# LayerNorm by a square root on ScalarE, pinned transposes and a shared last norm in a two-layer decoder trunk

## The chip, the core and the metric

The kernel runs on one core of one Trainium2 chip. A core has four compute engines, each with its own in-order instruction stream: TensorE (PE in the profile, with its weight loads as PEld) multiplies matrices into PSUM, VectorE (DVE) does elementwise work and statistics, ScalarE (ACT) does activations, scaled copies and casts, GpSimd (POOL) does a little elementwise work and issues DMAs. SyncE (SP) issues most DMAs. The engines meet through semaphores only. The metric is the device time of one execution in microseconds (us); the time before is the median of three runs.

## What is computed

Two layers over a sequence of 512 positions and a model width of 1024, in float32. Layer 0 mixes tokens with gated linear attention (GLA), layer 1 with a gated DeltaNet (GDN); a gated ConvFFN of inner width 2816 follows each. Every sublayer ends in the same way, so there are four LayerNorms:

```python
def layer_norm(x, g, b):
    xf = x.astype(jnp.float32)
    mu = jnp.mean(xf, -1, keepdims=True)
    var = jnp.mean(jnp.square(xf - mu), -1, keepdims=True)
    return ((xf - mu) * lax.rsqrt(var + LN_EPS)).astype(x.dtype) * g + b

h = x
for i in range(DEPTH):                       # DEPTH = 2
    y = gla_mixer(...) if i == 0 else gdn_mixer(...)
    h = layer_norm(ALPHA * h + y, ln_g[i, 0], ln_b[i, 0])
    h = layer_norm(ALPHA * h + conv_ffn(h, ...), ln_g[i, 1], ln_b[i, 1])
return h
```

## The kernel before

**Data and tiles.** The residual stream `h` is kept by token: four token blocks (`tb` 0 to 3) of 128 tokens, each in two halves (`hf`) of 512 columns, so a tile is 128 x 512. The input of every projection, `xh` and `xl`, is the same data transposed (features in the partitions), split in a rounded high part and a remainder; weights are split in the same way (`wh`, `wl`), and each product is three fast matmuls: high by high, high by low, low by high. `fm` products give the output by feature (128 features x 512 tokens), `tm` products by token.

**Stages.** GLA, its output projection and first LayerNorm; FFN of layer 0 and its LayerNorm; GDN, output projection and LayerNorm; FFN of layer 1 and the last LayerNorm, whose result goes to the output. A LayerNorm in the middle (`ln`, L698) normalizes a token block, transposes it on TensorE in eight 128 x 128 pieces (`tr4` into an `xT` bank), and writes `xh` and `xl` for the next stage. The next stage starts with four weight items on token blocks 0 and 1 alone and then does their second halves, so blocks 2 and 3 may come later. The last one (`ln_out`, L752) works in place: subtract the mean and multiply by the gain in one VectorE instruction (L757), scale and add the bias in a second (L758), for each half, then a DMA to the output (L759) on SP's queue.

**The statistics.** `ln_stats` (L680) takes mean and variance from `bn_stats` and `bn_aggr`, and gets the inverse square root on VectorE alone: a first value by integer arithmetic on the bits (L690), and three Newton steps of two instructions each (L693, L694) on 128 x 1 operands. It is one chain of nine small instructions, each of which needs the one before.

**Weights.** A plan lists every weight tile in the order of use. `prefetch` (L350) issues items up to `look` ahead of the one in use: SP's DMA into one of three `raw` buffers, ScalarE's rounding cast (L331, L276, L316) and VectorE's remainder (L332, L277, L317). Ordinary items are held to four at a time; the last projection of an FFN (`last_proj`, L864) keeps all its weights in 16 slots (`wsh`, `wsl`) instead. The letter `l` in the order of the FFN's last part raises `look` from 3 to 8; before, it stands ahead of the last four items.

**The last projection.** Token block by token block and half by half, four 128-row pieces of three matmuls each, 24 matmuls for a block. After a half VectorE adds the product to `h` (L879) and takes statistics (L880). After a block, its LayerNorm is spawned as a task.

**Order.** The program is traced once in Python; a running estimate `clk` of TensorE's time decides where in the trace a waiting task (a generator) goes on: `yield x` means not before x us of that estimate. Then a scheduler orders each engine's instructions; it may let an instruction pass earlier ones that it takes to be later. `keep_in_program_order` pins an instruction behind the one traced just before it on its engine. `pin` holds for the first projections of GLA alone, so the later transposes and matmuls are free. `table` puts ScalarE instructions that need a table of functions in one order among themselves; GLA's and the FFN's functions are not in that chain.

Of the kernel before, what the change touches and what calls it, by code (L numbers as in the profile page):

```python
# [42 lines left out]
CONV_DELAY = 6.0  # L43
COLS_DELAY = 64.0
# [9 lines left out]
def blk(i, n=P):  # L54
    return slice(i * n, i * n + n)


class Trunk:
# [3 lines left out]
    def __init__(self, ctx, tc):  # L62
# [117 lines left out]
    def tr(self, out, a, n=P):  # L180
        self.clk += 0.11
        t = self.nc.tensor.transpose(out, a, self.ident[:n, :n])  # L182
        if self.pin:
            self.tc.keep_in_program_order(t)

    def tr4(self, out, a):
        for j in range(4):
            self.tr(out[:, blk(j)], a[:, blk(j)])
# [248 lines left out]
    def tm_terms(self, ps, ah, al, wh, wl, first, last):  # L437
        self.mm(ps, ah, wh, first, False)
        self.mm(ps, ah, wl, False, False)
        self.mm(ps, al, wh, False, last)  # L440
# [239 lines left out]
    def ln_stats(self, tb):  # L680
        nc = self.nc
        mv = self.small([P, 2], "ln_mv")
        nc.vector.bn_aggr(mv, self.st[tb])
        hv = self.small([P, 1], "ln_var")
        nc.vector.tensor_scalar(hv, mv[:, 1:2], LN_EPS, 0.5, op0=ALU.add, op1=ALU.mult)

        rs = self.small([P, 1], "ln_rs")
        t = self.small([P, 1], "ln_t")
        ri = rs.bitcast(I32)
        nc.vector.tensor_scalar(ri, hv.bitcast(I32), -0.5, float(0x5F3759DF - 0x400000 - (1 << 31)),  # L690
                                op0=ALU.mult, op1=ALU.add)
        for _ in range(3):
            nc.vector.scalar_tensor_tensor(t, rs, hv, rs, ALU.mult, ALU.mult)  # L693
            nc.vector.scalar_tensor_tensor(rs, t, 1.5, rs, ALU.subtract, ALU.mult)  # L694
        self.vec(2.0)
        return mv, rs

    def ln(self, tb, spill=False):  # L698
# [53 lines left out]
    def ln_out(self, tb, out):  # L752
        nc = self.nc
        gb, h = self.ln_gb(), self.h[tb]
        mv, rs = self.ln_stats(tb)
        for hf in range(2):
            nc.vector.scalar_tensor_tensor(h[hf], h[hf], mv[:, 0:1], gb[hf], ALU.subtract, ALU.mult)  # L757
            nc.vector.scalar_tensor_tensor(h[hf], h[hf], rs, gb[2 + hf], ALU.mult, ALU.add)  # L758
            nc.sync.dma_start(out[blk(tb), blk(hf, S)], h[hf])  # L759
        yield 0.0  # L760
# [67 lines left out]
    def ffn(self, cw, li, g, b, final, out=False):  # L828
# [3 lines left out]
        for p0, p1 in CHUNKS + (PLAIN,):  # L832
# [31 lines left out]
    def last_proj(self, xs, final):  # L864
# [52 lines left out]
    def gates(self, nw, width, sg):  # L917
# [50 lines left out]
    def gla(self, li, g, b):  # L968
# [10 lines left out]
        def lr_done(ps):  # L979
            self.exp_ln_table()  # L980
# [154 lines left out]
    def mixer_out(self, y, li, g, b, final=None):  # L1135
# [6 lines left out]

        self.out_proj(a, NC, True, self.ln)
# [37 lines left out]
    def gdn(self, li, g, b):  # L1181
# [17 lines left out]
        def ba_done(ps):  # L1199
            self.exp_ln_table()  # L1200
# [410 lines left out]
```

## Time and profile before

| what | value |
|---|---|
| median of three runs | 1275.92 us (1275.64, 1279.84, 1275.92) |
| the profiled execution's own time | 1275.38 us |
| its span, first to last instruction | 1273.7 us |
| TensorE clock granted, mean | 0.997 of full |
| table loads on ScalarE | 10, of 1283 ns each |
| DMA traffic | 159.07 MB, mean 125 GB/s |

The profile page gives each engine's busy time and the costliest groups of instructions; other views of the same trace list the waits, the chain of work that ended last, or all instructions of an engine in order of time. A row of the time line gives the start in us, the duration in us, engine, source line, operation, output and inputs by the program's names, and in square brackets the idle time of the engine before it and what ended it. Source lines are those of the kernel printed above; L171 is the helper that issues every matmul and L182 the one that issues every transpose, so the tile's name (`fm`, `tm`, `xT`) tells which it is. Durations of TensorE's matmuls overlap: a 512-column matmul shows 0.39 us, but they follow each other every 0.227 us.

### The profile page before, as it was taken

What the parts mean: (1) busy time and instruction counts of PE and PEld (TensorE: products, weight loads), DVE (VectorE), ACT (ScalarE), POOL (GpSimd) and SP (SyncE); (2) the same over time, 40 slices, a digit from 0 to 9 for tenths busy, and PEclk for the clock granted to TensorE, in tenths of its full rate; (3) what the DMA queues carried; (4) which work ended last, traced back from release to release, by engine and by line L of the source; (5) the groups of instructions that cost most, each with busy time, mean ns of one, the idle gap of its engine ahead of it and who ended that gap; (6) DMA issues with size and microseconds to landing.
All of it is one profiled execution on the core that took longest, in us unless ns stands there. A gap on an engine that the chain in (4) does not pass through costs nothing.

```text
span 1273.7 us, 17779 instructions
## 1 busy us (share of the span) xinstructions
PE 1248.6 (98%) x6558; PEld 1049.4 (82%) x6558; DVE 872.3 (68%) x1704; ACT 612.4 (48%) x1176; POOL 153.0 (12%) x226
## 2 busy tenths in 40 slices
PE   8999999999999999999999999999999999999996
PEld 6878888988888888888888878888898888888885
DVE  3683366588667666686789955569777766766678
ACT  3553443554454544445766544443554454554440
POOL 4000000012201201101013130010011211211200
PEclk9999999999999999999999999999999999999998
DMA  7422224069757757742344331143249766756821
GB/s 184 114 71 66 67 84 148 2 151 223 171 132 181 155 129 182 162 130 73 100 145 112 110 95 34 60 124 91 75 108 217 158 160 155 162 150 151 212 83 66
DMA packets 182646, 159.07 MB, mean 125 GB/s; under 512 B 18328, under 2 KB 141786, under 8 KB 182560
## 3 DMA queue, kind: packets, MB, share of 16 engines
q1 hardware_dynamic: 161728, 114.05, 30.2%
q0 software_dynamic: 19440, 42.06, 18.0%
q10 hardware_dynamic: 1392, 1.84, 0.4%
q8 instruction: 51, 0.84, 0.3%
q14 instruction: 35, 0.29, 0.1%
HBM read 141.65 MB, written 5.78 MB: 116 GB/s over the span
## 4 chain that ended last, share of the span: by engine, by line
PE 83%; DVE 6%; DMA 2%; ACT 1%; issue 1%; DVEq 0%; ACTq 0%; SPq 0%
PE fm L171 44%; PE tm L171 30%; PE o L171 2%; PE R L171 1%; PE xT L182 1%; PE V L171 1%; DVE conv L1176 1%; DVE wl L332 1%; PE vn L171 1%; PE pg L171 1%; PE yT L182 1%; PE qkT L182 1%; PE s L171 0%; PE qs L171 0%; PE ks L171 0%
## 5 line engine op out<-in xcount | busy, mean ns | idle before, releaser
L171 PE MATMUL fm<-xh,wh 128*128 128x512 f32 (+1 forms) x1104 | 406.0, 368 | 0.7 <-ACT wh L331 0.7
L171 PE MATMUL fm<-xl,wh 128*128 128x512 f32 (+1 forms) x1104 | 402.5, 365 | 0.0
L171 PE MATMUL fm<-xh,wl 128*128 128x512 f32 (+1 forms) x1096 | 398.8, 365 | 2.6 <-DVE wl L332 2.6
L332 DVE TENSOR_TENSOR wl<-raw,wh 128x1024 fp32r<-128x1024 f32 (+1 forms) x134 | 162.5, 1214 | 142.7 <-ACT wh L331 141.5
L171 PEld LDWEIGHTS fm<-xh,wl 128*128 128x128 f32 x1096 | 206.2, 189 | 36.6 <-DVE wl L332 3.2
L171 PEld LDWEIGHTS fm<-xh,wh 128*128 128x128 f32 x1104 | 208.1, 188 | 34.2 <-ACT wh L331 1.6
L331 ACT CAST wh<-raw 128x1024 fp32r<-128x1024 f32 (+1 forms) x134 | 139.9, 1045 | 199.9 <-PE fm L171 109.8
L171 PEld LDWEIGHTS fm<-xl,wh 128*128 128x128 f32 x1104 | 208.2, 189 | 32.1
L825 DVE SCALAR_TENSOR_TENSOR conv<-fm,ffn_cw,conv 128x511 f32<-128x511 f32 (+1 forms) x176 | 131.0, 745 | 16.5 <-ACT conv L823 14.5
L276 ACT CAST wh<-wq 128x512 fp32r<-128x512 f32 x126 | 74.7, 619 | 107.0 <-PE fm L171 37.4
L277 DVE TENSOR_TENSOR wl<-wq,wh 128x512 fp32r<-128x512 f32 x126 | 84.7, 685 | 56.5 <-ACT wh L276 56.0
L234 POOL DMA_DIRECT2D wq<-in_ffn_w_out_dram x72 | 63.0, 902 | 260.6 <-DVE wl L277 152.1
L171 PE MATMUL tm<-wh,gh 128*128 128x512 f32 x216 | 84.0, 389 | 0.0
L171 PE MATMUL tm<-wl,gh 128*128 128x512 f32 x216 | 84.0, 389 | 0.0
L171 PE MATMUL tm<-wh,gl 128*128 128x512 f32 x216 | 84.0, 389 | 0.0
L171 PE MATMUL tm<-wh,xh 128*128 128x512 f32 x192 | 80.2, 418 | 1.0 <-ACT qk L992 1.0
L171 PE MATMUL tm<-wh,xl 128*128 128x512 f32 x192 | 75.3, 392 | 0.0
L171 PE MATMUL tm<-wl,xh 128*128 128x512 f32 x192 | 75.1, 391 | 0.0
L327 POOL DMA_DIRECT2D wl<-raw x20 | 17.2, 858 | 443.4 <-ACT wl L326 426.9
L531 DVE TENSOR_TENSOR h<-h,tm 128x512 f32<-128x512 f32 x68 | 44.8, 681 | 36.1 <-PE tm L171 36.1
L823 ACT ACTIVATE conv<-fm,ffn_cw 128x512 f32<-128x512 f32 x88 | 59.8, 682 | 0.0
L1176 DVE SCALAR_TENSOR_TENSOR conv<-fm,gdn_cw,conv 128x509 f32<-128x509 f32 (+2 forms) x72 | 53.3, 744 | 1.3 <-ACT conv L1174 0.7
(297 smaller groups left out, 1859.1 us busy)
## 6 DMA issues: line engine op xcount, KB each, us to landing
raw<-in_ffn_w_in_dram SPq DMA_DIRECT2D x88, 512.0 KB, 4.8
wq<-in_ffn_w_out_dram SPq DMA_DIRECT2D x72, 256.0 KB, 5.6
wq<-in_ffn_w_out_dram POOLq DMA_DIRECT2D x72, 256.0 KB, 4.8
raw<-in_gdn_w_in_dram SPq DMA_DIRECT2D x32, 512.0 KB, 4.1
raw<-in_gla_w_in_dram SPq DMA_DIRECT2D x23, 512.0 KB, 3.7
wl<-raw POOLq DMA_DIRECT2D x20, 512.0 KB, 4.7
raw<-in_gla_w_out_dram SPq DMA_DIRECT2D x8, 512.0 KB, 3.6
h<-in_ln_b_dram POOLq DMA_DIRECT2D x16, 256.0 KB, 7.3
```

The costliest lines, as they stand in the source:

```text
L171: t = self.nc.tensor.matmul(out, a, b, start=start, stop=stop, skip_group_check=open_group)
L182: t = self.nc.tensor.transpose(out, a, self.ident[:n, :n])
L234: nc.gpsimd.dma_start(t[i], quad(i, r, col), accum_op=ALU.add)
L276: nc.scalar.copy(wh, t)
L277: nc.vector.tensor_sub(wl, t, wh)
L327: nc.gpsimd.dma_start(wl.bitcast(F32), raw, accum_op=ALU.add)
L331: nc.scalar.copy(wh[:, cols], raw[:, cols])
L332: nc.vector.tensor_sub(wl[:, cols], raw[:, cols], wh[:, cols])
L531: nc.vector.tensor_tensor(h, h, banks[bank][j], op)
L823: nc.scalar.activation(a, ps, AF.Identity, scale=tap(2))
L825: nc.vector.scalar_tensor_tensor(a[:, d:], ps[:, :S - d], tap(2 - d), a[:, d:], ALU.mult, ALU.add)
L1176: self.conv = nc.vector.scalar_tensor_tensor(a[:, d:], ps[:, :S - d], tap(3 - d), a[:, d:], ALU.mult, ALU.add)
```

## The change

- **Statistics.** ScalarE takes the square root of the variance plus epsilon (a Sqrt activation whose bias is a new constant tile `eps`); VectorE takes the reciprocal and refines it by one Newton step instead of three. The estimate for the tasks (`vec`) is 1.2 in place of 2.0.
- **Tables.** The function table that has Sqrt is loaded ahead of each LayerNorm: before `out_proj` in both mixers, and before the last projection of both FFNs. Gelu, and Silu of the gates, join the `table` chain.
- **Order.** The transposes of `ln` and all matmuls of `last_proj` are pinned behind what is traced before them on TensorE. The transposes are traced 1.2 us of the estimate after the block is due (`LN_LAG`) instead of 0.2.
- **Weights.** The letter `l` stands ahead of the last eight items of the FFN instead of the last four.
- **The end.** For token blocks 0 and 1 the last LayerNorm is divided anew: ScalarE normalizes both halves (scale and bias), VectorE multiplies by the gain, a DMA on GpSimd's queue adds the bias row from DRAM, and SP's DMA writes the output. Blocks 2 and 3 stay as they were.

```diff
+LN_LAG = 1.2
...
+        self.eps = ones[:, 2:3]
         nc.gpsimd.memset(ones, 1.0)
+        nc.gpsimd.memset(self.eps, LN_EPS)
...
-    def tr(self, out, a, n=P):
+    def tr(self, out, a, n=P, order=False):
         self.clk += 0.11
         t = self.nc.tensor.transpose(out, a, self.ident[:n, :n])
-        if self.pin:
+        if self.pin or order:
             self.tc.keep_in_program_order(t)
...
-    def exp_ln_table(self):
-        load = self.nc.scalar.preload_act_table_set("natural_log_exp_and_others")
+    def act_table(self, name="natural_log_exp_and_others"):
+        load = self.nc.scalar.preload_act_table_set(name)
         self.tc.keep_in_program_order(load)
         self.table(load)
...
-        hv = self.small([P, 1], "ln_var")
-        nc.vector.tensor_scalar(hv, mv[:, 1:2], LN_EPS, 0.5, op0=ALU.add, op1=ALU.mult)
-
-        rs = self.small([P, 1], "ln_rs")
-        t = self.small([P, 1], "ln_t")
-        ri = rs.bitcast(I32)
-        nc.vector.tensor_scalar(ri, hv.bitcast(I32), -0.5, float(0x5F3759DF - 0x400000 - (1 << 31)),
-                                op0=ALU.mult, op1=ALU.add)
-        for _ in range(3):
-            nc.vector.scalar_tensor_tensor(t, rs, hv, rs, ALU.mult, ALU.mult)
-            nc.vector.scalar_tensor_tensor(rs, t, 1.5, rs, ALU.subtract, ALU.mult)
-        self.vec(2.0)
+        rs, hv, t = (self.small([P, 1], x) for x in ("ln_rs", "ln_var", "ln_t"))
+        self.table(nc.scalar.activation(rs, mv[:, 1:2], AF.Sqrt, bias=self.eps))
+        nc.vector.tensor_scalar(hv, mv[:, 1:2], LN_EPS, -0.5, op0=ALU.add, op1=ALU.mult)
+        nc.vector.reciprocal(rs, rs)
+        nc.vector.scalar_tensor_tensor(t, rs, hv, rs, ALU.mult, ALU.mult)
+        nc.vector.scalar_tensor_tensor(rs, t, 1.5, rs, ALU.add, ALU.mult)
+        self.vec(1.2, self.clk + 1.6)
         return mv, rs
...
-        yield ready - self.clk + 0.2
+        yield ready - self.clk + LN_LAG
         for hf in range(2):
             ps = self.psum("xT")
-            self.tr4(ps, h[hf])
+            self.tr4(ps, h[hf], True)
...
         mv, rs = self.ln_stats(tb)
+        if tb < 2:
+            nb = self.small([P, 1], "ln_nb")
+            nc.vector.scalar_tensor_tensor(nb, mv[:, 0:1], -1.0, rs, ALU.mult, ALU.mult)
+            for hf in range(2):
+                nc.scalar.activation(h[hf], h[hf], AF.Identity, bias=nb, scale=rs)
+                nc.vector.tensor_mul(h[hf], h[hf], gb[hf])
+                nc.gpsimd.dma_start(h[hf], self.gb_rows[1][blk(hf, S)].partition_broadcast(P), accum_op=ALU.add)
+                nc.sync.dma_start(out[blk(tb), blk(hf, S)], h[hf])
+            return
...
-                    nc.scalar.activation(a, a, AF.Gelu)
+                    self.table(nc.scalar.activation(a, a, AF.Gelu))
...
-            self.fm_items(items, steps, order[:-4] + "l" + order[-4:] if plain else order)
+            self.fm_items(items, steps, order[:-8] + "l" + order[-8:] if plain else order)
...
         self.drain()
+        self.act_table("sqrt_and_others")
         self.ln_begin(li, g, b)
...
-                    self.tm_terms(ps, *(t[:, blk(tb)] for t in xs[c]), *ws[hf][c], c == 0, c == n - 1)
+                    self.tm_terms(ps, *(t[:, blk(tb)] for t in xs[c]), *ws[hf][c], c == 0, c == n - 1, True)
...
-                nc.scalar.activation(t, ps, AF.Silu)
+                self.table(nc.scalar.activation(t, ps, AF.Silu))
...
+        self.act_table("sqrt_and_others")
         self.out_proj(a, NC, True, self.ln)
```

More of the change, by code (lines that the diff above doesn't have):

```diff
@@ L178, in vec, with tr4 @@
         return self.dve
-    def tr(self, out, a, n=P):
+    def tr(self, out, a, n=P, order=False):
         self.clk += 0.11
         t = self.nc.tensor.transpose(out, a, self.ident[:n, :n])
-        if self.pin:
+        if self.pin or order:
             self.tc.keep_in_program_order(t)
-    def tr4(self, out, a):
+    def tr4(self, out, a, order=False):
         for j in range(4):
-            self.tr(out[:, blk(j)], a[:, blk(j)])
+            self.tr(out[:, blk(j)], a[:, blk(j)], order=order)
     def mm4(self, out, a, b):
@@ L434, in fm_items, with tm_terms @@
             raise RuntimeError
[L437 to L440, printed above, removed]
+    def tm_terms(self, ps, ah, al, wh, wl, first, last, order=False):
+        self.mm(ps, ah, wh, first, False, order=order)
+        self.mm(ps, ah, wl, False, False, order=order)
+        self.mm(ps, al, wh, False, last, order=order)
     def tm_half(self, a, n, tail, done, slots=False):
@@ L979, in lr_done @@
         def lr_done(ps):
-            self.exp_ln_table()
+            self.act_table()
             nc.scalar.copy(lr[:96, :], ps[:96, :])
@@ L1199, in ba_done @@
         def ba_done(ps):
-            self.exp_ln_table()
+            self.act_table()
             self.table(nc.scalar.activation(ba[:8, :], ps[:8, :], AF.Exp, scale=-1.0))
```

## The prediction

> **What bounds the kernel now.** The page first (engines, share of the span), then the view of TensorE's waits, then the end in order of time.
>
> ```profile
> span 1273.7 us, 17779 instructions
> PE 1248.6 (98%) x6558; PEld 1049.4 (82%) x6558; DVE 872.3 (68%) x1704; ACT 612.4 (48%) x1176; POOL 153.0 (12%) x226
> ...
> PE xT L182 <- DVE h L708: 2.9, 2, 2.7
> PE xT L182 <- DVE ln_rs L694: 0.6, 1, 0.6
> PE tm L171 <- ACT gh L573: 0.2, 1, 0.2
> ```
>
> TensorE is busy for 98% of the span. The change takes no matmul away, so only time in which TensorE stands can be won: 1273.7 - 1248.6 = 25.1 us. Of the waits listed, those at a LayerNorm (transposes `xT`, and one cast at the last projection) are 2.9 + 0.6 + 0.2 = 3.7 us. The largest other part is the end:
>
> ```profile
> 1261.89 0.39 PE L171 MATMUL tm<-wsh,gl 128*128 128x512 f32 x1
> ...
> 1268.98 1.42 DVE L758 SCALAR_TENSOR_TENSOR h<-h,ln_rs,gb 128x512 f32<-128x512 f32 x2
> ...
> 1217.40 5.44 PE tm L171 x24
> ...
> 1255.00:1260.00 5.00, 5.00 (x19) 1.00 0.00 0
> 1260.00:1265.00 5.00, 5.00 (x16) 1.00 0.28 105
> 1265.00:1270.00 5.00, 4.79 (x14) 0.58 0.28 105
> ```
>
> The last matmul ends at 1262.28, VectorE's last instruction at 1270.40, the span at 1273.7: TensorE is done 11.4 us before the end, and VectorE fills nearly all of the stretch (5.00, 5.00 and 4.79 us of 5). Its last result leaves by DMA in the remaining 3.3 us, which the change leaves alone. So two things can be won: at most 3.7 us inside, and VectorE's backlog at the end. The profiled execution took 1275.38 us, 0.54 below the median of 1275.92; 1.7 us of it lie outside the span. I work against 1275.38.
>
> **The end.** VectorE's groups over 1246 to 1274 (busy us, mean ns), and the nearest rows for what is new:
>
> ```profile
> L757 DVE SCALAR_TENSOR_TENSOR h<-h,ln_mv,gb 128x512 f32<-128x512 f32 x8 | 5.9, 741 | 0.0
> L758 DVE SCALAR_TENSOR_TENSOR h<-h,ln_rs,gb 128x512 f32<-128x512 f32 x8 | 5.6, 747 | 0.1
> L880 DVE BATCH_NORM_STATS2 ln_st<-h 128x6 f32<-128x512 f32 x7 | 4.8, 690 | 0.1
> L879 DVE TENSOR_TENSOR h<-h,tm 128x512 f32<-128x512 f32 x7 | 4.7, 675 | 1.3 <-PE tm L171 1.3
> L693 DVE SCALAR_TENSOR_TENSOR ln_t<-ln_rs,ln_var 128x1 f32<-128x1 f32 x12 | 2.5, 209 | 0.1
> L694 DVE SCALAR_TENSOR_TENSOR ln_rs<-ln_t,ln_rs 128x1 f32<-128x1 f32 x12 | 1.8, 153 | 0.2
> L683 DVE BATCH_NORM_AGGREGATE ln_mv<-ln_st 128x2 f32<-128x12 f32 x4 | 0.8, 209 | 0.1
> ...
> L1269 DVE RECIPROCAL gd_bp<-gd_bp 128x4 f32<-128x4 f32 x8 | 1.3, 172 | 0.1
> L744 DVE TENSOR_TENSOR h<-h,gb 128x512 f32<-128x512 f32 x16 | 10.8, 684 | 1.4 <-DMA gb<-in_ln_g_dram 1.4
> L707 ACT ACTIVATE h<-h,ln_nb,ln_rs 128x512 f32<-128x512 f32 x12 | 9.8, 818 | 30.4 <-DVE ln_nb L706 30.3
> L1209 ACT ACTIVATE gd_ea<-gdn_al 8x1 f32<-8x1 f32 x1 | 0.2, 187 | 0.0
> ```
>
> A token block costs VectorE now (4.8 + 4.7) / 7 x 2 = 2.7 us of adds and statistics, (5.9 + 5.6) / 4 = 2.9 of normalizing, (2.5 + 1.8) / 4 = 1.1 of Newton steps, 0.2 for L683 and 0.3 for two more small ones (taken like L694): 7.2 us, while TensorE brings a block every 5.44. Hence the backlog. Afterwards the small chain is one instruction for the variance (0.15), the reciprocal (0.17), 0.21 and 0.15: 0.7. Blocks 0 and 1 pay 2.7 + 0.2 + 0.7 + 0.16 + two multiplications like L744, 1.36: 5.1 us, under TensorE's 5.44. Blocks 2 and 3 pay 2.7 + 0.2 + 0.7 + 2.9 = 6.5.
>
> The halves of the last projection end every 2.72 us, so block 2's first half is there at 1262.28 - 3 x 2.72 = 1254.1. What VectorE still owes block 1 by then I put at 1.4 us (its small chain, ScalarE's 0.82 and the two multiplications begin at about 1252.8), and VectorE isn't idle after: 1254.1 + 1.4 + 2 x 6.5 = 1268.5 against 1270.40, a gain of **1.9 us**. The bounds: no backlog at all when TensorE ends, then block 3's own chain after its second half is 1.4 + 0.2 + 0.7 + 2.9 = 5.2 and VectorE ends at 1267.4, a gain of 3.0; or the scheduler leaves gaps where VectorE waits for ScalarE, half of it, 0.8. The Sqrt isn't in the trace; the 0.19 us of L1209 is the nearest (a 128 x 512 activation, 0.82, the upper end), and VectorE has block work to put under it. ScalarE does nothing at the end now, so the two 0.82 us normalizations for each block are free there. The bias adds of blocks 0 and 1 and the four outputs are weighed as a rival.
>
> **Start of GDN.** TensorE's longest wait in the change's reach:
>
> ```profile
> 565.32 0.50 PE L171 MATMUL tm<-wsh,gh 128*128 128x512 f32 x1 [0.18 <-ACT gh L573]
> 574.27 0.39 PE L171 MATMUL tm<-wsh,gl 128*128 128x512 f32 x1
> 577.35 1.09 PE L182 MATMUL xT<-ident,h 128*128 128x128 f32 x8 [2.69 <-DVE h L708]
> ...
> 565.93 0.68 DVE L574 TENSOR_TENSOR gl<-conv,gh 128x512 fp32r<-128x512 f32 x1
> 573.08 0.20 DVE L683 BATCH_NORM_AGGREGATE ln_mv<-ln_st 128x2 f32<-128x12 f32 x1
> 574.70 0.69 DVE L879 TENSOR_TENSOR h<-h,tm 128x512 f32<-128x512 f32 x1
> 576.75 0.54 DVE L708 TENSOR_SCALAR h<-h,ln_mv,ln_rs 128x512 f32<-128x512 f32 x1
> ```
>
> Block 0's statistics are done at 573.28, its normalized half at 577.29: 4.0 us, because nine small instructions alternate with block 1's adds and statistics. With the Sqrt the chain alone is 0.25 for ScalarE and the hand-over, 0.6 for the reciprocal and one step, 0.16 and 0.54: done at about 574.9, or 576.3 if two of block 1's 0.69 us instructions stand between. The pins take something back: today TensorE runs past the products that need `gl`, written at 566.61; pinned, it stands there from about 565.8, 0.8 us, and reaches the transposes at 575.4 and not at 574.66. So they start at 575.4 to 576.3 and not at 577.35: a gain of 1.0 to 1.9, I take **1.4**. `LN_LAG` decides the place in TensorE's order: behind block 1's 24 matmuls, where the row shows the transposes already.
>
> **Start of the second FFN.**
>
> ```profile
> 903.11 0.63 PE L182 MATMUL xT<-ident,h 128*128 128x128 f32 x4 [0.56 <-DVE ln_rs L694]
> 899.38 0.21 DVE L683 BATCH_NORM_AGGREGATE ln_mv<-ln_st 128x2 f32<-128x12 f32 x1
> 902.42 0.54 DVE L708 TENSOR_SCALAR h<-h,ln_mv,ln_rs 128x512 f32<-128x512 f32 x1
> ```
>
> Here the chain takes 899.38 to 902.96; the short one, even with two 0.69 us instructions between, 3.1 us and so half a microsecond less. TensorE was free at 902.55: the wait of 0.56 goes, **0.6**. After GLA no transposes wait long enough to be listed: 0.
>
> **Weights sooner: 0.** The first of these loads is asked for long before its cast:
>
> ```profile
> 525.87 0.53 SPq L302 DMA_DIRECT2D raw<-in_ffn_w_out_dram  x1
> raw<-in_ffn_w_out_dram SPq DMA_DIRECT2D x8, 512.0 KB, 3.9
> ...
> 550.72 0.62 ACT L276 CAST wh<-wq 128x512 fp32r<-128x512 f32 x1 [4.07 <-issue]
> 551.83 1.65 ACT L316 CAST wsh<-raw 128x512 fp32r<-128x512 f32 x3
> ```
>
> The cast at 551.83 is 26 us behind the issue, and the median landing takes 3.9, so the load isn't late: the cast stands behind L276, and that one for a buffer. Only four ordinary items may be held, and the extra items of `look` come after those, so the letter moves little: the casts are traced one item sooner. Were they to fill ScalarE's gap of 4.07 us, VectorE's work ahead of block 0's statistics would shrink and the rest of the 2.69 could go; the bounds are 0 and 1.3, and a slot taken sooner could delay a convolution by one 0.69 us instruction. I take 0, as the queue's order is kept.
>
> **Tables.** Four loads more, on an engine that is 52% idle:
>
> ```profile
> 2.21 1.28 ACT L638 ACT_TABLE_LOAD   x1 [2.21 <-issue]
> 3.51 0.19 ACT L638 COPY one<-one 128x1 f32<-128x1 f32 x1
> ```
>
> A load costs 1.28 us, and the copy follows 0.02 us after. Its cover is ScalarE's idle time; if one stands ahead of the cast of `gh` (565.32, where TensorE waits already) it costs up to 1.28 there once. The Trainium skill, "ScalarE: Activation LUTs", section "What ACT_TABLE_LOAD costs", adds a drain of 1380 ns to the load's 1283; the row of the copy shows none, and by the page that one misplaced load would cost 2.66, an estimate.
>
> **Sum.** 1.9 + 1.4 + 0.6 = 3.9 us: 1275.38 - 3.9 = **1271.5**.
>
> **The rivals.**
> - *What is won inside is given back.* The pins hold TensorE at `gl` and at transposes that come too soon, and only the end is won: 1275.4 - 1.9 = 1273.5. For it: the 0.8 us above; against: the chain is shorter by four instructions everywhere.
> - *All of it.* The 3.7 us inside go whole and the end gains 3.0, about 6.5 in all: 1268.9. It needs the casts in the gap and a well-chosen order on VectorE.
> - *Slower: the Sqrt stands in ScalarE's queue.* Between stages ScalarE runs eight scaled copies for a block in a row:
>
> ```profile
> 235.16 2.90 ACT L717 ACTIVATE xf<-xT,lb,lg 128x128 f32<-128x128 f32 x8 [0.46 <-PE xT L182]
> ...
> DMA to landing us min/median/max: 5.9/7.3/10.3
> ```
>
> A Sqrt behind such a run is 2.9 us late; VectorE's queue stands at the reciprocal, and pinned transposes make TensorE stand too. It decides from where the delay exceeds the chain's saving of about 1 us and the half-stage of cover; at worst 2.9 after GLA and after GDN: 1275.4 + 5.8 - 3.3 = 1277.9. Against it: block 3's copies there end near the time at which the old chain ended.
> - *The output queue.* SP's queue is in order, and blocks 2 and 3 leave behind block 1, which now waits for its bias add: multiplied at about 1256, landed at 1263 (7.3, the median of the row of landings above, for these adds of the bias in earlier norms) to 1266.3 (10.3), before block 3's first half at 1267.8. Only past that does it cost; landed at 1270, it gives about 1274. The Trainium skill, "SBUF — State Buffer", section "Who interferes with whom", says that a VectorE instruction in a two-port mode locks GpSimd out, descriptors included, so that these adds would land later; no row here shows the last stretch with them.
> - *It doesn't do what it says*: the order on VectorE is again the limit, 1275.4.
>
> **How the numbers follow.** Forecast 0.57, given back 0.20, all of it 0.12, Sqrt in the queue 0.06, output queue 0.03, unchanged 0.02. About 0.5% is what a measurement of this kernel can tell from no change: 1269.5 to 1282.3 around the median. Faster than that are the second rival and the forecast's lower edge, 0.15; slower only if the queue costs more than worked out, 0.03; same 0.82. The range takes in both ends of the end's gain (0.8 to 3.0) and of the inside (0 to 3.7), up to the unchanged case and a median half a microsecond above the profiled run: 1268.0 to 1276.0.
>
> **What would show it.** VectorE's last instruction ends at about 1266.5 (1268.5 less the 2.0 won before); the wait at the start of GDN falls from 2.7 to 1 to 2 us in all (the part at `gl` is new), that at 903 is gone; nine small instructions are five, with a Sqrt of about 0.2 us. Wrong would be: new waits of TensorE for ScalarE, transposes that stand over 1 us elsewhere, outputs of blocks 2 and 3 issued late behind block 1.

## The result and the profile after

The changed kernel took 1267.04 us (median of 6 runs, 1266.18 to 1269.06), the kernel before, run beside it, 1275.78 (median of 6, 1274.37 to 1279.84). The ratio is 0.9929, with a 95% interval of 0.9914 to 0.9944: faster by 0.7%, 8.7 us. The forecast was 1271.5, a gain of 3.9, and its range of 1268.0 to 1276.0 does not hold the time. The profiled execution of the changed kernel took 1266.89 us, its span is 8.5 us shorter than that of before.

The page after, engines and span:

```profile
span 1265.2 us, 17748 instructions
PE 1247.4 (99%) x6558; PEld 1049.5 (83%) x6558; DVE 863.3 (68%) x1638; ACT 624.2 (49%) x1200; POOL 155.3 (12%) x231
```

And the whole view of TensorE's waits (total, times, longest, in us):

```profile
PE warm L629 <- POOL reset L87: 2.0, 1, 2.0
PE fm L174 <- DVE wl L335: 1.8, 2, 1.3
PE cols L185 <- DMA rows<-in_gdn_conv_w_dram: 1.1, 1, 1.1
PE qkT L185 <- ACT conv L1187: 1.1, 2, 0.7
PE tm L174 <- ACT qk L1000: 1.0, 1, 1.0
PE V L174 <- DMA T<-dinvt: 0.8, 1, 0.8
PE R L174 <- issue: 0.6, 1, 0.6
PE tm L174 <- DVE gl L577: 0.3, 1, 0.3
```

The reader is to see what is missing: no transposition `xT` waits any more. Of the 3.7 us of waits at the LayerNorms, 0.3 is left, at `gl`, where the pins were expected to cost 0.8.

To place the gain, TensorE's instructions were counted in the order of their starts; there are 6558 in every profile. The stages below are the times between the starts of two of them: "GLA's norm" from the 1001st to the 1401st, "GDN" (FFN's last projection, its LayerNorm and the start of GDN) from the 2501st to the 2901st, "second FFN" (GDN's output projection, its norm, the FFN's start) from the 4701st to the 5061st. "Start" is the start of the 161st, long before any LayerNorm, and "end" runs from the start of the last product to the end of the span.

| us | start | GLA's norm | GDN | second FFN | end | span |
|---|---|---|---|---|---|---|
| before | 30.71 | 66.91 | 81.60 | 63.92 | 11.77 | 1273.7 |
| changed | 29.37 | 66.51 | 78.69 | 62.69 | 9.30 | 1265.2 |
| gain | 1.34 | 0.40 | 2.91 | 1.23 | 2.47 | 8.5 |
| forecast | 0 | 0 | 1.4 | 0.6 | 1.9 | 3.9 |

The columns leave out the stretches in between, which agree within 0.1 us in these two profiles. Every part of the forecast is too small, GDN the most. The time line of the changed kernel at the start of GDN, TensorE first and then VectorE:

```profile
564.14 0.50 PE L174 MATMUL tm<-wsh,gl 128*128 128x512 f32 x1 [0.34 <-DVE gl L577]
572.67 0.60 PE L185 MATMUL xT<-ident,h 128*128 128x128 f32 x4
...
568.87 0.21 DVE L686 BATCH_NORM_AGGREGATE ln_mv<-ln_st 128x2 f32<-128x12 f32 x1
570.16 0.54 DVE L706 TENSOR_SCALAR h<-h,ln_mv,ln_rs 128x512 f32<-128x512 f32 x1
```

Block 0's chain now takes 568.87 to 570.70 where it took 573.08 to 577.29: it is 2.4 us shorter, and it also begins 4.2 us sooner, of which the stages ahead explain only 1.7 (0.40 and the start's 1.34). So something ahead of the statistics has gone too, and the small chain cannot be the reason. The transposes begin at 572.67 without a wait, 2 us after their input.

### The profile page after: what moved, and what is told of

It reads as the page before. It is cut to its first block, busy times and chain, and to the rows that moved or that the text cites. A ratio compares the mean times of both kernels' runs of the same rounds, so it can differ in the third digit from the quotient of the medians.

```text
span 1265.2 us, 17748 instructions
## 1 busy us (share of the span) xinstructions
PE 1247.4 (99%) x6558; PEld 1049.5 (83%) x6558; DVE 863.3 (68%) x1638; ACT 624.2 (49%) x1200; POOL 155.3 (12%) x231
## 4 chain that ended last, share of the span: by engine, by line
PE 87%; DVE 4%; ACT 1%; DMA 1%; issue 0%; DVEq 0%; ACTq 0%; SPq 0%
PE fm L174 46%; PE tm L174 31%; PE o L174 2%; PE R L174 1%; PE xT L185 1%; PE V L174 1%; DVE conv L1185 1%; DVE wl L335 1%; PE vn L174 1%; PE pg L174 1%; PE yT L185 1%; PE qkT L185 1%; PE s L174 0%; PE qs L174 0%; PE ks L174 0%
```

## The experiments

Each kernel is the one named with the edit shown (e12 has two); all were run in five rounds beside the kernel before. This table has the stages of their profiles (us), the median of the times and the ratio to before; the text goes through them. The same kernel profiled again (e1 and the changed one; e5 and before) shows the three inner stages and the end within 0.1 us, so these are read to a tenth or two, and far better than the times can be. The table has no column for the stretch from the second FFN's to the last product: it takes 332.5 to 332.7 us, but 332.9 in e2 and in e8 and 333.1 in e11.

| run | start | GLA's norm | GDN | second FFN | end | median | ratio, 95% interval |
|---|---|---|---|---|---|---|---|
| e1 changed, again | 28.20 | 66.50 | 78.62 | 62.66 | 9.30 | 1265.78 | 0.9930 (0.9918 to 0.9943) |
| e2 letter back | 28.05 | 66.51 | 80.15 | 62.67 | 9.30 | 1268.29 | 0.9946 (0.9934 to 0.9959) |
| e3 old end | 29.57 | 66.51 | 78.58 | 62.66 | 10.10 | 1268.18 | 0.9944 (0.9931 to 0.9956) |
| e4 old statistics | 30.51 | 66.67 | 78.45 | 64.40 | 11.55 | 1271.57 | 0.9968 (0.9956 to 0.9980) |
| e5 before, again | 30.34 | 66.93 | 81.66 | 63.89 | 11.77 | 1276.24 | 0.9999 (0.9990 to 1.0008) |
| e6 before, letter alone | 30.48 | 66.92 | 78.36 | 63.94 | 11.76 | 1271.67 | 0.9967 (0.9955 to 0.9980) |
| e7 before, statistics alone | 27.62 | 66.58 | 80.61 | 64.36 | 10.11 | 1271.19 | 0.9964 (0.9951 to 0.9978) |
| e8 before, memset alone | 30.57 | 66.93 | 82.93 | 64.05 | 11.76 | 1275.54 | 0.9998 (0.9988 to 1.0008) |
| e9 before, table loads alone | 28.43 | 66.93 | 81.70 | 63.79 | 11.78 | 1274.83 | 0.9997 (0.9987 to 1.0007) |
| e10 changed, no pins | 29.51 | 66.50 | 78.33 | 62.67 | 9.30 | 1266.65 | 0.9927 (0.9914 to 0.9939) |
| e11 changed, lag back | 29.88 | 66.58 | 78.76 | 64.09 | 9.30 | 1269.19 | 0.9947 (0.9934 to 0.9959) |
| e12 no pins, lag back | 28.31 | 66.58 | 78.11 | 64.00 | 9.29 | 1268.17 | 0.9937 (0.9925 to 0.9949) |
| e13 a stop of 2.2 us | 28.25 | 66.50 | 78.71 | 65.00 | 9.30 | 1268.96 | 0.9949 (0.9936 to 0.9963) |
| e14 a stop of 5.3 us | 29.51 | 66.51 | 78.80 | 69.60 | 9.31 | 1274.11 | 0.9986 (0.9977 to 0.9995) |

### The letter: e2 and e6

The changed kernel with the letter at its old place, and the kernel before with the letter at its new one:

```diff
-            self.fm_items(items, steps, order[:-8] + "l" + order[-8:] if plain else order)
+            self.fm_items(items, steps, order[:-4] + "l" + order[-4:] if plain else order)
```

> The changed kernel with the letter for the last projection's weights four places from the end again, as before the change. TensorE's order stays, only the order of the casts on ScalarE and VectorE differs. Theory A (the prediction: weights sooner are worth nothing, the shorter chain alone brings the inside): 1267.0, the transposes at the start of GDN begin with no wait to speak of. Theory B (the earlier casts clear VectorE ahead of block 0's statistics and bring the 1.5 us that the prediction lacked): 1268.5, and a wait of TensorE for VectorE of 1 to 1.6 us is back at the start of GDN; at the start of the second FFN nothing, since its tail is another line of code; at the end of the kernel nothing.

> The kernel before with one edit alone: the letter for the last projection's weights eight places from the end. With the new statistics and pins it was worth 1.5 us at the start of GDN (from product 2501 to 2901: 81.60 us before, 80.15 with the letter put back, 78.69 changed) and 0.4 at the second FFN's end (58.63 against 58.25 from product 6301). Theory A (the casts alone clear VectorE, so that the old chain is in time as well, as it was with the old statistics in the changed kernel, 78.45): the stage at GDN takes 78.4 to 78.8, the time falls by about 3: 1272.5. Theory B (the pins are needed for it): 80 to 81, and 1274.

Put back (e2), it costs 1.5 us at GDN, and some 0.4 us late in the second FFN; put in alone (e6), it gains 3.2 at GDN and changes no other stage. That is theory B of e2 and theory A of e6. TensorE of e2 at the start of GDN:

```profile
562.67 0.50 PE L174 MATMUL tm<-wsh,gh 128*128 128x512 f32 x1 [0.71 <-ACT gh L576]
564.01 0.50 PE L174 MATMUL tm<-wsh,gl 128*128 128x512 f32 x1 [0.61 <-DVE gl L577]
572.70 0.66 PE L185 MATMUL xT<-ident,h 128*128 128x128 f32 x4
```

The waits are not at the transposes, where the reason given in e2's theory B would put them, but 9 to 10 us sooner, at the casts of the last activations: `gh` on ScalarE and `gl` on VectorE come late. They stand behind the casts of weights. This is the remainder of the last projection's weights (`wsl`) on VectorE, as a group: its eight instructions with the shortest, median and longest duration in ns and the first and the last start, in the kernel before, in e6 and in the changed kernel:

```profile
L317 DVE TENSOR_TENSOR wsl<-raw,wsh x8: 678/680/682, 552.6 to 559.9; 128x512 fp32r<-128x512 f32 x8
```

```profile
L317 DVE TENSOR_TENSOR wsl<-raw,wsh x8: 681/684/694, 545.3 to 553.9; 128x512 fp32r<-128x512 f32 x8
```

```profile
L320 DVE TENSOR_TENSOR wsl<-raw,wsh x8: 678/682/691, 543.8 to 552.1; 128x512 fp32r<-128x512 f32 x8
```

With the letter at eight the eight remainders are through by 554.6, not by 560.6: what follows in the two queues, GDN's own weight casts and the split of the last convolution, is done sooner too, and so the statistics begin sooner. The last of GDN's four remainders on VectorE, which stands right ahead of block 0's additions and statistics, in the kernel before and in e6:

```profile
568.96 1.22 DVE L332 TENSOR_TENSOR wl<-raw,wh 128x1024 fp32r<-128x1024 f32 x1
```

```profile
566.02 1.22 DVE L332 TENSOR_TENSOR wl<-raw,wh 128x1024 fp32r<-128x1024 f32 x1
```

It is 2.9 us sooner, and the statistics 3.2. ScalarE's time line of the kernel before shows that the later loads were late indeed (the prediction looked at the first of them only):

```profile
558.45 1.14 ACT L316 CAST wsh<-raw 128x512 fp32r<-128x512 f32 x2 [2.18 <-DMA raw<-in_ffn_w_out_dram]
```

In e6 the nine small instructions of the old chain are all there, and TensorE's transposes hardly wait (they start 0.40 us behind the product ahead of them, where 0.23 is usual):

```profile
569.92 0.21 DVE L683 BATCH_NORM_AGGREGATE ln_mv<-ln_st 128x2 f32<-128x12 f32 x1
572.96 0.54 DVE L708 TENSOR_SCALAR h<-h,ln_mv,ln_rs 128x512 f32<-128x512 f32 x1
573.55 0.66 PE L182 MATMUL xT<-ident,h 128*128 128x128 f32 x4
```

The chain ends at 573.50, 3.6 us after the aggregate, where it took 4.2 before, but it starts 3.2 us sooner.

### The statistics: e4 and e7

e4 is the changed kernel with the old statistics (three Newton steps, no Sqrt, no loads of its table, the old estimate of 2.0); its edit is shown, shortened. e7 is the kernel before with the new statistics, their estimate and their table loads:

```diff
-        self.table(nc.scalar.activation(rs, mv[:, 1:2], AF.Sqrt, bias=self.eps))
-        nc.vector.tensor_scalar(hv, mv[:, 1:2], LN_EPS, -0.5, op0=ALU.add, op1=ALU.mult)
-        nc.vector.reciprocal(rs, rs)
-        nc.vector.scalar_tensor_tensor(t, rs, hv, rs, ALU.mult, ALU.mult)
-        nc.vector.scalar_tensor_tensor(rs, t, 1.5, rs, ALU.add, ALU.mult)
-        self.vec(1.2, self.clk + 1.6)
...
+        for _ in range(3):
+            nc.vector.scalar_tensor_tensor(t, rs, hv, rs, ALU.mult, ALU.mult)
+            nc.vector.scalar_tensor_tensor(rs, t, 1.5, rs, ALU.subtract, ALU.mult)
+        self.vec(2.0)
...
-        self.act_table("sqrt_and_others")
```

> The changed kernel with the three Newton steps on VectorE in place of the Sqrt, the reciprocal and one step, and without the loads of the Sqrt's table; pins, LN_LAG, the earlier weights and the shared end stay. Theory A (the statistics carry the inside): the waits at the starts of GDN and of the second FFN come back by about 2 us each or less, and the end loses about 0.7 for each of blocks 2 and 3: 1269 to 1271. Theory B (pins and earlier weights carry the inside): the inside stays, the end loses 1 to 1.5 alone: 1268 to 1268.5.

> The kernel before with the new statistics alone (Sqrt on ScalarE, reciprocal and one step on VectorE, the table loads); no pins, LN_LAG 0.2, the letter at four, the old end. Theory A (terms add up as the runs so far have them): 0.2 after GLA, 1.4 at the start of GDN as the prediction had it, 0.6 to 1.2 at the second FFN, 1.7 at the end, 3.9 to 4.5 together: 1271 to 1271.5. Theory B (the prediction's reason for pins: without them the scheduler's order lets TensorE stand at transposes whose inputs it thinks ready, and takes the inside back): only the end's 1.7 is left: 1273.8.

e4 is a mixture: GDN keeps its whole gain with the old chain (78.45, theory B there), the second FFN loses 1.7 (theory A), and the end loses 2.25, more than either said. In e7 the time is what theory A said (1271.19), but for a wrong reason: its start is the earliest of all, 27.62, and its stages gain only 0.33 + 0.99 + 1.66 and lose 0.44 at the second FFN, 2.5 together; two stretches between them lose 0.5 more. A time that fits is no proof of the sum behind it; the stages are.

TensorE of e7, at the starts of GDN and of the second FFN, and VectorE's reciprocal of block 1:

```profile
572.95 1.09 PE L184 MATMUL xT<-ident,h 128*128 128x128 f32 x8 [1.31 <-DVE h L705]
...
898.61 0.63 PE L184 MATMUL xT<-ident,h 128*128 128x128 f32 x4 [1.44 <-DVE ln_mv L685]
...
576.76 0.16 DVE L689 RECIPROCAL ln_rs<-ln_rs 128x1 f32<-128x1 f32 x1 [0.43 <-ACT ln_rs L687]
```

The shorter chain alone halves GDN's stop (2.69 to 1.31). At the second FFN the transposes now wait 1.44 us, more than the 0.56 before: with the smaller estimate the task is traced sooner, and its first transposes stand six products sooner in TensorE's order (the 4865th instruction in place of the 4871st), ahead of products that could have run. The last row is the rival "the Sqrt stands in ScalarE's queue", seen. ScalarE's time line of e7:

```profile
573.64 2.91 ACT L714 ACTIVATE xf<-xT,lb,lg 128x128 f32<-128x128 f32 x8 [0.36 <-PE xT L184]
576.40 0.33 ACT L687 ACTIVATE ln_rs<-ln_mv,one 128x1 f32<-128x1 f32 x1
```

Block 1's aggregate was done at 573.74, its Sqrt began 2.7 us later, behind eight scaled copies; TensorE did not wait for that block's transposes, which stand at 580.05.

### Pins and lag: e10, e11 and e12

```diff
-            self.tr4(ps, h[hf], True)
+            self.tr4(ps, h[hf])
...
-                    self.tm_terms(ps, *(t[:, blk(tb)] for t in xs[c]), *ws[hf][c], c == 0, c == n - 1, True)
+                    self.tm_terms(ps, *(t[:, blk(tb)] for t in xs[c]), *ws[hf][c], c == 0, c == n - 1)
```

is e10; e11 has the next edit instead, and e12 both.

```diff
-LN_LAG = 1.2
+LN_LAG = 0.2
```

> The changed kernel without the pins: the transposes of the norms and the products of the last projection are the scheduler's to place again; LN_LAG stays 1.2. Theory A (the prediction: pinned, TensorE stands at gl): the wait of 0.2 to 0.3 at the start of GDN goes, its stage takes 78.3 to 78.5 in place of 78.7, the rest is as it was: 1266.5. Theory B (the pins keep the transposes where LN_LAG puts them, and carry the second FFN's 1.2 us, which the new statistics alone lost again, 64.36): that stage takes 64 or more: 1268.3.

> The changed kernel with LN_LAG at 0.2 as before, pins and all else as changed. Theory A (the lag is what places the transposes behind block 1's products; at 0.2 they come too soon and, pinned, hold TensorE up): waits at the transposes come back, the second FFN's stage takes 64.0 to 64.6 in place of 62.7, GDN's 79.5 to 81 in place of 78.7: 1269.5 to 1271. Theory B (the shorter chain and the earlier casts make it in time at either lag): as changed, 1267.

> The changed kernel without pins and with LN_LAG at 0.2: the new statistics, the earlier weights and the shared end are left of the change. Theory A (the pins turn a wrong lag into a wait; without them the scheduler moves other products ahead): GDN's stage 78.5 to 79.5, the second FFN's 64.0 to 64.4 as with the statistics alone: 1268.5 to 1269.5, and less than with pins and the lag at 0.2. Theory B (pins do nothing either way, the lag all): the same as with pins and the lag at 0.2.

Without pins (e10) GDN is 0.3 shorter and nothing else changes: theory A. TensorE's order differs at one product, the first with `gl`, which stands two products later and no longer waits. With the lag at 0.2 (e11) the second FFN loses its gain and 0.2 more, GDN does not: half of theory A. With neither (e12) GDN is at its shortest, 78.11, and the second FFN loses as in e11. So the lag, not the pins, carries the second FFN. What it does there is to keep a place: the first transposes of that stage are TensorE's 4871st instruction before the change, after it and in e4; with the smaller estimate of the new statistics and the old lag (e7, e11, e12) they are the 4865th, and wait. e11 loses 0.6 us more behind that stage, e12 does not, so at the old lag the pins cost something; why, no run shows. TensorE at the second FFN's start in the changed kernel, in e11, and in e4, which has the lag but not the short chain:

```profile
897.39 0.40 PE L174 MATMUL tm<-wsh,yl 128*128 128x512 f32 x1
897.63 0.60 PE L185 MATMUL xT<-ident,h 128*128 128x128 f32 x4
```

```profile
898.20 0.63 PE L185 MATMUL xT<-ident,h 128*128 128x128 f32 x4 [1.16 <-DVE ln_mv L686]
```

```profile
899.31 0.63 PE L185 MATMUL xT<-ident,h 128*128 128x128 f32 x4 [0.72 <-DVE ln_rs L697]
```

Either part alone makes this stage longer than before (64.0 to 64.4 against 63.9), both together 1.2 us shorter. e10 is as fast as the changed kernel within what can be measured; none of the versions is faster than that.

### The end: e3

The branch for token blocks 0 and 1 is taken out of `ln_out`:

```diff
         mv, rs = self.ln_stats(tb)
-        if tb < 2:
-            nb = self.small([P, 1], "ln_nb")
...
-            return
```

> The changed kernel with all four blocks of the last LayerNorm on VectorE again; the new statistics stay. Theory A (the prediction: a block costs VectorE 6.5 us against TensorE's 5.44, so a backlog of about 2 us for two blocks comes back): VectorE's last instruction ends 1 to 2 us later, 1268 to 1269. Theory B (the shorter chain alone has cleared the backlog, sharing adds nothing): 1267.0 to 1267.3. Theory C (sharing brought all 2.5 us): 1269.5.

By the median (1268.18) theory A; by the end's column 0.8 us come back, between A and B. VectorE's last two instructions and TensorE's last product, in the changed kernel and in e3:

```profile
1260.49 1.42 DVE L765 SCALAR_TENSOR_TENSOR h<-h,ln_rs,gb 128x512 f32<-128x512 f32 x2
...
1255.88 0.39 PE L174 MATMUL tm<-wsh,gl 128*128 128x512 f32 x1
```

```profile
1261.39 1.42 DVE L756 SCALAR_TENSOR_TENSOR h<-h,ln_rs,gb 128x512 f32<-128x512 f32 x2
...
1255.96 0.39 PE L174 MATMUL tm<-wsh,gl 128*128 128x512 f32 x1
```

From start to start VectorE is 4.61 us behind in the changed kernel, 5.43 in e3, and was 7.09 before (1268.98 - 1261.89). With the end column of the table: the new statistics alone gain 1.66 (e7), the shared end alone, with old statistics, 0.22 (e4), both 2.47. With the long chain ScalarE gets its part later; VectorE's first multiplication of e4 waits for it three times as long as in the changed kernel (0.28), 0.6 us more, which is about what the shared end loses there (0.22 in place of the 0.80 of e3):

```profile
1247.93 0.69 DVE L764 TENSOR_TENSOR h<-h,gb 128x512 f32<-128x512 f32 x1 [0.88 <-ACT h L763]
```

### The start: e1, e5, e8 and e9

The changed kernel and the kernel before, unchanged; the kernel before with one memset more (e8), and with the table loads alone (e9; its memset and its Gelu and Silu in the `table` chain are not shown):

```diff
         nc.gpsimd.memset(ones, 1.0)
+        nc.gpsimd.memset(ones[:, 2:3], 2.0)
```

```diff
         self.drain()
+        self.act_table("sqrt_and_others")
...
+        self.act_table("sqrt_and_others")
         self.out_proj(a, NC, True, self.ln)
```

> The changed kernel once more, unchanged. Its profile had TensorE's first gate products (fm) start at 10.37 us, 0.75 earlier than before, and 1.33 us in all were gone before any LayerNorm had run, though the orders of the two kernels differ there by one small memset on GpSimd alone. Theory A (the landing of the first loads varies from run to run): the start here lies anywhere between 10.3 and 11.2 us, and the time between 1266.2 and 1268.5. Theory B (the memset, or a place in memory, brings it): the start is 10.4 again, and 1267.0.

> The kernel before, once more and unchanged. Theory A (the start varies from run to run, whatever the kernel): TensorE's 161st product, at 30.71 us in the profile of before and at 28.05 to 30.51 in those of the changed kernel and of its variants, begins anywhere between 28 and 31, and the times have their median near 1275.5. Theory B (the change brings the start forward): it begins at 30.5 or later again.

> The kernel before with one memset more of 128x1 on GpSimd, at the place where the change sets the epsilon (its value, 2.0, is read by nothing). Theory A (the start varies by itself): as before, 1275.5, the 161st product anywhere between 28 and 31 us. Theory B (the memset shifts the loads of the start): the 161st product begins at 28 to 29.5, and the time falls by 1 to 1.5: 1274.2.

> The kernel before with its Newton steps, and with the table loads alone: the Sqrt's table is asked for where the change does, nothing uses it, and the silu and gelu tables are loaded again after it; the epsilon's memset is there too. The five profiles with the new statistics start at 27.6 to 29.6 us (TensorE's 161st product), the five with Newton steps at 30.3 to 30.7. Theory A (the additional table set is what lets the first loads land sooner): 28 to 29.6 here. Theory B (it is something else about the statistics, or chance): 30.3 to 30.7. Of the loads themselves both expect what the prediction said, nothing at any stage: 66.9 after GLA, 81.6 at the start of GDN, 63.9 at the second FFN, 11.77 from the last product's start to the end; a load in the wrong place would add up to 1.3 to one of them.

The start moved by 1.34 us between the two first profiles, and in 16 profiles of kernels with the same order up to there it lies between 27.6 and 30.7 us. It is not the memset (e8, 30.57). Five of the six with Newton steps lie at 30.34 to 30.71, the ten with the Sqrt at 27.62 to 29.88. The sixth is e9, at 28.43, as its theory A said; but its times differ from those of before by nothing that can be measured (0.9997), so one profile's start says little about a kernel. The first loads are asked for at the same time and land later or sooner: the load of GLA's weights that is asked for at 2.74 us took 15.9 us before and 11.6 in e7. This stays open: it may be variation from run to run alone, or a shift of up to 1 us that goes with the program. e9 also shows that the four table loads cost nothing: all its stages are those of before.

### What a stop costs beyond itself: e13 and e14

The inside and the end are 7.0 us, the medians are 8.7 apart (9.7 in e1). e8's profile shows one reason, in the view of windows (stretch; length and busy time of each engine; the third number from the right is the granted clock of TensorE):

```profile
90.00:95.00 5.00, 3.80 (x16) 2.46 (x15) 1.90 (x5) 1.63 (x2) 0.00 (x0) 0.93 0.27 101
...
575.00:580.00 5.00, 2.31 (x11) 1.66 (x10) 4.58 (x21) 0.82 (x1) 0.20 (x1) 0.90 0.22 65
580.00:585.00 5.00, 5.00 (x22) 4.33 (x21) 2.57 (x9) 4.11 (x10) 1.47 (x3) 0.76 0.44 161
```

The mean of 5 us hides the form of it: in windows of 1 us the clock is at 0.50 from 579 to 582 and at 0.81 in the next, and likewise at 0.50 from 95 to 97 with 0.64 ahead and 0.66 behind. So it is at half for 3.4 us, twice: once from 2.1 us after the beginning of the stop of 2.7 us at 577, and once 2.4 us behind a stop of 1.2 us at 91. GDN's stage is 1.3 us longer than in the other profiles with its order (82.93 against 81.60 to 81.70). The stop at 91, of 0.9 to 1.2 us, is in all 16 profiles, and only e8 shows a fall behind it; that it is the cause there is not shown. To see whether the stop is the cause, it was put into the changed kernel at another place, the second FFN's start, in two lengths (16 and 28 instructions):

```diff
+        if li == 2 and tb == 0:
+            for _ in range(16):
+                nc.vector.tensor_scalar(rs, rs, 1.0, 0.0, op0=ALU.mult, op1=ALU.add)
         nc.scalar.activation(h[1], h[1], AF.Identity, bias=nb, scale=rs)
```

> The changed kernel with 16 small VectorE instructions more (128x1, times 1.0 plus 0.0) in the chain of block 0's statistics at the second FFN's start, so that its transposes come later: a stop of TensorE of some 2 us there, where the changed kernel has none. Theory A (a stop of 2 us or more lets the granted clock fall for some us behind it, in some executions): the mean clock is 0.996 or lower in about half of the executions, as with the kernel before, and these cost 1.3 us beyond the stop: 1268.5 to 1271, widely spread. Theory B (the low clocks belong to something else of the kernel before): 0.997 to 0.999 in all, and the time is longer by the stop alone, 1268.5 to 1269.5.

> The same with 28 instructions: a stop of some 4 to 5 us. Theory A: low clocks in more than half of the executions, the clock of the stretch behind the stop at about 0.75 in the profile if it falls into one, 1271 to 1274. Theory B: clocks of 0.997 to 0.999, 1270.5 to 1272.

The stops came out at 2.2 and 5.3 us, as TensorE's time line shows for e13 and then for e14:

```profile
899.99 1.50 PE L185 MATMUL xT<-ident,h 128*128 128x128 f32 x12 [2.17 <-DVE h L709]
```

```profile
904.24 2.79 PE L185 MATMUL xT<-ident,h 128*128 128x128 f32 x12 [5.29 <-DVE ln_nb L704]
```

The windows at and behind them, of 5 us for e13:

```profile
895.00:900.00 5.00, 2.83 (x14) 2.04 (x12) 4.60 (x27) 1.81 (x3) 0.00 (x0) 1.00 0.17 50
900.00:905.00 5.00, 5.00 (x31) 4.36 (x32) 3.17 (x7) 4.46 (x14) 0.00 (x0) 1.00 0.02 3
```

and of 1 us for e14:

```profile
903.00:904.00 1.00, 0.00 (x0) 0.00 (x0) 1.00 (x7) 0.46 (x1) 0.00 (x0) 0.95 0.00 0
904.00:905.00 1.00, 0.76 (x4) 0.79 (x5) 0.62 (x3) 1.00 (x2) 0.00 (x0) 0.50 0.00 0
905.00:906.00 1.00, 1.00 (x7) 1.00 (x6) 0.00 (x0) 0.69 (x3) 0.00 (x0) 0.50 0.00 0
906.00:907.00 1.00, 1.00 (x6) 1.00 (x5) 0.10 (x1) 1.00 (x4) 0.00 (x0) 0.50 0.00 0
907.00:908.00 1.00, 1.00 (x6) 0.77 (x5) 0.96 (x2) 1.00 (x4) 0.00 (x0) 0.85 0.00 0
```

Behind 2.2 us the clock stays at 1.00, and the stage is longer by the stop alone (65.00 - 62.69 = 2.3). With 5.3 us it falls to half, again for 3.4 us, and the stage is 6.9 us longer (69.60 - 62.69), 1.6 more than the stop. Over all executions: a mean clock of 0.996 or lower was recorded in none of five of e13, in all eleven of e14, and in 38 of the 61 of the kernel before that ran beside these experiments, with its stop of 2.7 us. Of the kernels whose longest stop behind the start was 2.2 us or less, e13 among them, one execution in 57 shows it; e6, the kernel before with the letter's edit that takes the stop at GDN away, has 0.997 in all five. The times follow the clock: the kernel before took 1274.9 us in the mean of its 23 executions at 0.997, 1276.5 in the 21 at 0.995 and 1278.1 in the 12 at 0.994. So e14 came out as theory A had it (1274.11 is a little over its range), e13 as theory B: the chance of a fall is small at 2.2 us and over a half at 2.7, as far as stops at two places can be compared. That it would be a half at 2 us, as e13's theory A had it, was wrong.

## Why the prediction was wrong, point by point

- **Weights sooner: 0.** This is the step that failed: "the letter moves little: the casts are traced one item sooner", with bounds of 0 to 1.3. It was worth 3.2 us alone and 1.5 with the rest in place. The step rests on the first load, which was in time, and on the rule of four items; but the eight casts and eight remainders moved on two queues, by six microseconds on VectorE's (the groups above), and the last loads were late (2.18 us of ScalarE's idle time). The prediction named the way it came about, "VectorE's work ahead of block 0's statistics would shrink and the rest of the 2.69 could go", and set it to nothing.
- **Start of GDN: 1.4.** Without the letter the stage gains 1.45 (e2), so the sum was right, though not by its parts: the statistics alone gain 0.99 (e7). The terms do not add: 1.45 and 3.24 make 4.7, where the stops there were about 3.2, counted from start to start as in the next point. Either nearly removes the same stop; with the letter in place the old chain is as good as the new (78.45 against 78.69).
- **At most 3.7 us inside.** This limit was wrong too: GLA's norm, GDN and the second FFN gained 4.5. The waits listed begin at the end that the profile shows for the product ahead, 0.39 us after its start, but a product that waits for nothing starts 0.23 us after the one ahead. So each stop behind such a product costs 0.16 us more than its row says: GDN's is 577.35 - 574.27 - 0.23 = 2.85, not 2.69, and the one at `gh` 0.34, not 0.18.
- **Pins: 0.8 at `gl`.** Right in place, too large with the earlier casts: 0.34 in the changed kernel; 0.71 and 0.61 at `gh` and `gl` in e2. Taking the pins away gains 0.3.
- **Second FFN: 0.6.** The term was mis-sized, 1.23. Counted from start to start, the first transpose (903.11) stood 0.95 us behind the product ahead of it, 0.24 in the changed kernel: 0.71 and not 0.56. A second stop, ahead of a later block's transposes, has 0.18 in its row and 0.46 us from start to start (from 917.41), where 0.12 is usual. Neither is left; they make 1.05 of the 1.23. The prediction weighed the lag for GDN only, while it is here that the transposes would have come too soon without it. The two rows of before:

```profile
902.16 0.39 PE L171 MATMUL tm<-wsh,yl 128*128 128x512 f32 x1
...
917.87 0.66 PE L182 MATMUL xT<-ident,h 128*128 128x128 f32 x4 [0.18 <-DVE h L708]
```

- **After GLA: 0.** 0.40, of which 0.33 come with the statistics alone (e7). There was a stop too short for a row: before, transposes at 240.47 start 0.40 us behind the product ahead, where 0.12 is usual.
- **The end: 1.9.** The mechanism was right, the size 2.47, inside the bounds of 0.8 to 3.0. What VectorE owed block 1 was put at 1.4 and was 0.69 + 0.67. Blocks 2 and 3 were put at 6.5 each by summing durations; from block 2's first addition to VectorE's last instruction there are 1261.91 - 1248.24 = 13.7 us, less those 1.36 and so 6.2 each: shown durations of 0.67 to 0.75 us overlap, and instructions in a row start 0.6 to 0.7 us apart. These are the first addition and block 1's two multiplications:

```profile
1248.24 0.68 DVE L887 TENSOR_TENSOR h<-h,tm 128x512 f32<-128x512 f32 x1
1249.20 0.69 DVE L759 TENSOR_TENSOR h<-h,gb 128x512 f32<-128x512 f32 x1 [0.28 <-ACT h L758]
...
1250.42 0.67 DVE L759 TENSOR_TENSOR h<-h,gb 128x512 f32<-128x512 f32 x1
```

- **Tables: 0.** Right (e9). The Trainium skill, "ScalarE: Activation LUTs", section "What ACT_TABLE_LOAD costs", has a drain beside the load; no stage of e9 shows one, with four loads more, and the instruction behind a load starts 0.01 to 0.03 us after its end in twelve of fourteen cases.
- **The rivals.** "All of it" came nearest: inside and end gained 7.0 us where it had 6.5, and it named both conditions, the casts in the gap and VectorE's order; it had a chance of 0.12. Its 6.5 was partly luck: the inside gained 4.5, not 3.7, and the end 2.47, not 3.0. "Given back" was wrong: the pins cost 0.3. The Sqrt did stand in ScalarE's queue in e7, at a place that cost nothing. The output queue cost nothing either: the bias adds landed in 4.5 us at the median, not in 7.3 to 10.3 (the view of DMAs from 1240 us on; KB each, median us to landing), and the span ends 3.3 us behind VectorE's last instruction, as before:

```profile
h<-in_ln_b_dram POOLq DMA_DIRECT2D x4, 256.0 KB, 4.5
```

- **The start and the clock** stood in no term. The start's 1.3 us in the two profiles is open; a fall of the clock makes the times of before about 1.6 us longer in over half of its executions by their mean clocks; the profiled execution, without such a fall, does not show it. That it happens behind GDN's stop is seen in one profile, e8's, and inferred for the others.

## What to carry to other kernels

A request that moves in a program can move the casts behind it on every queue: find what stands ahead of the critical chain on its engine, last item as well as first, before such an edit is put at nothing. Count a stop from start to start where shown durations overlap; here the waits as listed were 3.7 us, and 4.5 were gained. Parts that shorten the same wait do not add, and parts that are useless alone (here a shorter chain, and a lag that keeps its consumer's place when the estimate of the chain shrinks) can be worth over a microsecond together, so they are to be priced and tried together. Where times of a kernel scatter by more than its stages do, compare stages of the traces, counted by the instructions of the busiest engine.

## What was not expected of the hardware

A stop of TensorE can cost more than its length: with one of 5.3 us the granted clock fell to half for 3.4 us (1.6 us more in that stage). With one of 2.7 us it did so in e8's profile (1.3 us more), and 38 of 61 executions of the kernel before have a mean clock that tells of a fall; with 2.2 us none of five has. Once, in e8, a fall came 2.4 us behind a stop of only 1.2 us. The Trainium skill, "TensorE: Matmul & The Clock Gate", section "HAM oscillation — how this bites in real kernels", warns of idle gaps over some 3.4 us; the runs here put the point lower, at or below 2.7, and the measurement decides. By the same page of the Trainium skill, section "What's actually happening", the window that it watches runs free of the kernel, which would make it a matter of chance at such lengths; no run here shows the window itself.
